# Adding expert results to their rows in DRAM by indirect accumulating transfers, in place of one-hot products

## The chip, the cores and the metric

The kernel runs on one core of a Trainium2 chip. Its time is the device time in microseconds. Three runs of the kernel before took 1575.61, 1576.45 and 1577.78, median 1576.45. Engines are named as in the profile: PE (TensorE, with PEld for its weight loads), DVE (VectorE), ACT (ScalarE), POOL (GpSimd), SP (SyncE). Transfers are issued from the queues of SP, ACT and POOL and carried out by 16 DMA engines.

## The reference

Two blocks run one after the other on a 512 x 1024 float32 activation. The first (mLSTM, convolution, feed-forward) and the attention parts of the second are not touched by the change. The last part of the second is a mixture of experts, and the change lies there:

```
def hierarchical_moe(h, w_group, b_group, w_expert, b_expert, w_gate, w_up, w_down):   # one row of 512 tokens
    g_sel = argmax(h @ w_group + b_group)                  # 1 of 4 groups per token
    e_logits = (h @ w_expert)[of the group]                # 8 experts in a group, 32 in all
    top_idx = top_k(e_logits + e_bias, 2)                  # 2 experts of that group per token
    gate = one_hot(g_sel) * normalised top-2 weights * g_w # 512 x 32
    a, u = h @ w_gate[e], h @ w_up[e]                      # 1024 -> 256 for each expert e
    return sum over e of (silu(a) * u * gate[:, e]) @ w_down[e]   # 256 -> 1024
```

Its result is added to the 512 x 1024 residual `x`. The two experts of a token always lie in the same group of eight.

## The kernel before, in words

`moe` (line 1557) holds the residual in four row tiles `xs[0..3]` of 128 tokens (each 128 x 1024, 512 KB; they lie in a buffer that the profile calls `crossq_U`). The output product `cross_w_o` of the cross attention ends with `fin0` and `fin1`, which add to `xs`, form the router's logits (line 1612), and store the normalised input of the experts, without its row scale, into the DRAM tensor `hd` (line 1618, from ACT's queue).

Then 16 expert pairs are worked through, pair p being experts 2p and 2p + 1. Each expert has 64 slots, so that a pair fills the 128 partitions. `pos` holds for each token and expert its slot, counted from 1, or 0. An expert with more than 64 tokens would be taken up again in `overflow`. For a pair, with the time at which it is called in iteration i of the loop (lines 1689 to 1703):

- `pair_take` (called for pair i + 3): `slots` compares `pos` with a ramp, which gives a one-hot matrix of tokens and slots; `look` multiplies it with `parts` (token number, gates and row scale, split into three bf16 parts), so each slot knows its token and gate. `fetch` gathers the 128 rows from `hd` by an indirect transfer of POOL's queue. An empty slot reads row 0. `pair_gates` sums the three parts.
- `pair_flip` (for pair i + 1): eight transposes on PE give `xT`.
- `pair_up` (pair i): 16 float32 matmuls of 512 columns, with gate and up weights side by side; then silu on ACT and a product on DVE. Inside, at k = 4 and 7, the results of the pair before are added to `xs[0]` and `xs[1]`.
- `pair_turn`: two transposes give `aT`. After it come the additions to `xs[2]` and `xs[3]`.
- `pair_down`: eight float32 matmuls give 128 x 1024; `split` writes the result as a rounded high part (ACT, line 188) and a low part (DVE, line 189) into `y`.
- `pair_add`: `pair_back` compares a ramp of token numbers with the token of each slot (line 1908); for each of the four row tiles and both halves two matmuls with this one-hot matrix (line 1901, high and low part) bring the slots back to their tokens, and DVE adds them to `xs` (line 1902). `pair_last` does it for the last pair by halves and stores the output (lines 1920 to 1922).

The weights of a pair are 12 pieces of 128 x 1024 float32 (512 KB): 8 of gate and up, 4 of down, in the order of their use (`ORDER`). `prefetch` issues them on SP's queue (line 1745) into a ring of places, piece n into place n modulo their number; a piece waits for the products that read the place before. Places become known step by step: 14 early, 11 in `hook`, 8 more before routing, 33 in all. The order on each engine is that in which the program calls these functions; nothing reorders it.

An accumulating transfer is also used in the first block: `weight` (line 138) writes a low part of a weight as copy of the negated high part (ACT) plus an accumulating transfer of the raw weight from SBUF to SBUF on POOL's queue, 512 KB each.

Of the kernel before, what the change touches and what calls it, by code (L numbers as in the profile page):

```python
# [11 lines left out]
F32 = mybir.dt.float32  # L12
F32R = mybir.dt.float32r
BF16 = mybir.dt.bfloat16
I32 = mybir.dt.int32
AF = mybir.ActivationFunctionType
ALU = mybir.AluOpType
PSUM = bass.MemoryType.PSUM

P = 128  # L20
S = 512
# [25 lines left out]
class Kern:  # L47
# [1509 lines left out]
    def moe(self, pm, o, X):  # L1557
# [24 lines left out]

        self.hd = self.dr.tile([S, D], F32, tag="hd", name="hd")

        info = self.info = pm.tile([P, 4, 34], F32, tag="info", name="info")
        self.parts = pm.tile([P, 4, 34, 3], BF16, tag="parts", name="parts")
        for tb in range(4):
            nc.gpsimd.iota(info[:, tb, 32:33], pattern=[[1, 1]], base=tb * P, channel_multiplier=1,
                           allow_small_or_imprecise_dtypes=True)
        self.split3(self.parts[:, :, 32:33], info[:, :, 32:33])  # L1590
        lg = pm.tile([P, 4, 36], F32, tag="lg", name="lg")

        half = {}

        def logits(tb, h):

            c = slice(h * 512, (h + 1) * 512)
            x = self.xs[tb][:, c]
            ss = self.small(1)
            self.sumsq(x, ss)  # L1600
            ps = self.psB()
            for k in range(4):
                nc.tensor.transpose(ps[:, k * P:(k + 1) * P], x[:, k * P:(k + 1) * P], self.ident)
            if tb == 3 and h == 1:
                dd = self.psB()
                for _ in range(1):
                    nc.tensor.matmul(dd[:, :256], self.ident, x[:, :256], start=True, stop=True)
            hT = pm.tile([P, 4, P], F32, tag="xg", bufs=2, name=self.nm("hT"))
            nc.scalar.copy(hT.rearrange("p k c -> p (k c)"), ps)
            pl = self.psB()  # L1610
            for k in range(4):
                nc.tensor.matmul(pl[:, :36], hT[:, k], wr[:, 4 * h + k], start=k == 0, stop=k == 3)
            if tb == 3 and h == 1:
                for _ in range(1):
                    nc.tensor.matmul(dd[:, :256], self.ident, x[:, :256], start=True, stop=True)
            t = self.tA()
            nc.vector.tensor_tensor(t, x, grow[:, c], op=ALU.mult)
            nc.scalar.dma_start(self.hd[tb * P:(tb + 1) * P, c], t)
            return ss, pl

        def fin0(tb, bank):
# [26 lines left out]
        def route(tbs):  # L1648
            self.places_of(tbs)
            t = slice(tbs[0], tbs[-1] + 1)  # L1650
            self.slots(oh[:, t], self.pos[:, t, 0:2])

        rest = Halves([])

# [22 lines left out]
        self.pair_collect(st[0], oh, (2, 3))  # L1677
        for p in range(3):
            st[p] = st.get(p, {})
            st[p]["oh"] = self.slots(self.slot_tile(), pos[:, :, 2 * p:2 * p + 2])  # L1680
            if p:
                self.fetch(st[p], self.look(st[p]["oh"], self.parts[:, :, 32:33]))
        self.gates_to(info[:, :, 0:32], pm, lg)
        self.split3(self.parts[:, :, 0:32], info[:, :, 0:32])
        self.split3(self.parts[:, :, 33:34], info[:, :, 33:34])
        for p in range(3):
            self.pair_gates(st[p], self.look(st[p]["oh"], self.parts), (2 * p, 2 * p + 1, 32))
        nwin = self.more_windows(pm, mb, onb)
        for i in range(16):
            prev = st.pop(i - 1) if i else None  # L1690
            self.pair_up(st[i], self.pair_weights(i), prev)
            self.prefetch(12 * i + 8)
            if i + 1 < 16:
                self.pair_flip(st[i + 1])
            self.pair_turn(st[i])
            if prev:
                self.pair_add(prev, (2, 3))
            if i + 3 < 16:
                p = i + 3
                st[p] = self.pair_take(pos[:, :, 2 * p:2 * p + 2], self.parts, (2 * p, 2 * p + 1, 32))  # L1700
            if i < 15:
                self.pair_down(st[i], self.pair_weights(i))
                self.prefetch(12 * (i + 1))
        for h in range(2):
            self.pair_down(st[15], self.pair_weights(15), (h,))
            self.pair_last(st[15], h)
# [18 lines left out]
    def prefetch(self, used):  # L1725

        a = self.a
        free = used + len(self.places)
        while len(self.pieces) < min(free, 192 if free >= 192 else 188):
            n = len(self.pieces)  # L1730
            if n == 188:

                for n in range(188, 192):
                    self.pieces.append(self.places[n % len(self.places)])
                for h in range(2):
                    for n in range(188, 192):
                        j, i = self.ORDER[n % 12]
                        c = slice(h * 512, (h + 1) * 512)
                        self.nc.sync.dma_start(self.pieces[n][:, c], a["w_dn"][30 + j, (i - 4) * P:(i - 3) * P, c])
                break  # L1740
            j, i = self.ORDER[n % 12]
            e = n // 12 * 2 + j
            src = a["w_gu"][e, i] if i < 4 else a["w_dn"][e, (i - 4) * P:(i - 3) * P, :]
            t = self.places[n % len(self.places)]
            self.nc.sync.dma_start(t, src)
            self.pieces.append(t)
# [17 lines left out]

    def slot_tile(self):
        return self.p0.tile([P, 4, 2, 64], BF16, tag="tB", bufs=4, name=self.nm("oh"))

    def slots(self, oh, pos):

# [26 lines left out]
    def fetch(self, s, tk):  # L1796

        nc = self.nc
        tf = self.small(1)
        nc.vector.tensor_reduce(tf, tk, axis=mybir.AxisListType.X, op=ALU.add)  # L1800
        ti = self.small(1, dt=I32)
        nc.vector.tensor_copy(ti, tf)
        xg = s["xg"] = self.pm.tile([P, 1024], F32, tag="xg", bufs=2, name=self.nm("xg"))
        nc.gpsimd.indirect_dma_start(out=xg, out_offset=None, in_=self.hd,
                                     in_offset=bass.IndirectOffsetOnAxis(ap=ti, axis=0))

    def pair_gates(self, s, ps, cols):

        nc = self.nc
        X = mybir.AxisListType.X  # L1810
        gt = s["gt"] = self.p0.tile([P, 3], F32, tag="gt", bufs=5, name=self.nm("gt"))
        nc.vector.tensor_reduce(gt[:, 1:3], ps[:, cols[2]:cols[2] + 2], axis=X, op=ALU.add)
        for j in range(2):
            r = slice(64 * j, 64 * j + 64)
            nc.vector.tensor_reduce(gt[r, 0:1], ps[r, cols[j]:cols[j] + 1], axis=X, op=ALU.add)
        nc.vector.tensor_tensor(gt[:, 0:1], gt[:, 0:1], gt[:, 2:3], op=ALU.mult)

    def pair_take(self, pos, parts, cols):

# [30 lines left out]
    def pair_flip(self, s):  # L1850
        s["xT"] = self.flip(s["xg"])

    def pair_up(self, s, w, prev=None):

        nc, pm = self.nc, self.pm
        ps = self.psA()
        for k in range(8):
            if prev and k in (4, 7):
                self.pair_add(prev, (0 if k == 4 else 1,))
            for j in range(2):  # L1860
                r = slice(64 * j, 64 * j + 64)
                nc.tensor.matmul(ps[r, :], s["xT"][:, k, r], w[j][k // 2][:, (k % 2) * 512:(k % 2 + 1) * 512], start=k == 0, stop=k == 7)  # L1862
        sl = pm.tile([P, 256], F32, tag="sl", bufs=2, name=self.nm("sl"))
        nc.scalar.activation(sl, ps[:, :256], AF.Silu, scale=s["gt"][:, 2:3])  # L1864
        nc.vector.scalar_tensor_tensor(sl, sl, s["gt"][:, 0:1], ps[:, 256:], op0=ALU.mult, op1=ALU.mult)
        s["sl"] = sl
# [7 lines left out]
        aT = s["aT"] = pm.tile([P, 2, P], F32, tag="aT", bufs=2, name=self.nm("aT"))  # L1874
        nc.vector.tensor_copy(aT.rearrange("p a b -> p (a b)"), pt[:, :256])

    def pair_down(self, s, w, hs=(0, 1)):
        nc, pm = self.nc, self.pm
        if hs[0] == 0:
            s["y"] = pm.tile([P, 2, 1024], F32R, tag="y", name=self.nm("y"))  # L1880
        y = s["y"]
        pd = {h: self.psA() for h in hs}
        for f in range(2):
            for h in hs:
# [2 lines left out]
                    nc.tensor.matmul(pd[h][r, :], s["aT"][:, f, r], w[j][4 + f][:, h * 512:(h + 1) * 512], start=f == 0, stop=f == 1)  # L1887
        for h in hs:
            c = slice(h * 512, (h + 1) * 512)
            self.split(y[:, 0, c], y[:, 1, c], pd[h])  # L1890

    def pair_add(self, s, tbs=range(4)):

# [50 lines left out]
    def overflow(self, pm, nwin):  # L1944
# [3 lines left out]
        with tc.If(n > 0):  # L1948
            pd = self.dr.tile([16, P, 4, 6], F32, tag="pd", name="pd")
            st = pm.tile([P, 4, 6], F32, tag="ofst", bufs=2, name="ofst")  # L1950
            for p in range(16):
                nc.vector.tensor_copy(st[:, :, 0:2], self.pos[:, :, 2 * p:2 * p + 2])
                nc.vector.tensor_copy(st[:, :, 2:4], self.info[:, :, 2 * p:2 * p + 2])
                nc.vector.tensor_copy(st[:, :, 4:6], self.info[:, :, 32:34])
                nc.sync.dma_start(pd[p], st)
            base = pm.tile([P, 1], F32, tag="base", name="base")
            nc.vector.memset(base, 0.0)
            with tc.For_i(0, n, 1):
                nc.vector.tensor_scalar(base, base, 64.0, None, op0=ALU.add)
                with tc.For_i(0, 16, 1) as p:  # L1960
# [3 lines left out]
                    for j in range(2):  # L1964
                        for i in range(6):
                            t = self.places[j * 6 + i]
                            if i < 4:
                                src = a["w_gu"][bass.ds(2 * p + j, 1), i]
                            else:
                                src = a["w_dn"][bass.ds(2 * p + j, 1), (i - 4) * P:(i - 3) * P]  # L1970
                            nc.sync.dma_start(t, src.rearrange("a p c -> (a p) c"))
                            ow[j][i] = t
                    nc.vector.tensor_scalar(st[:, :, 0:2], st[:, :, 0:2], base, None, op0=ALU.subtract)
# [144 lines left out]
```

## Time and profile before

| | us |
|---|---|
| median of three runs | 1576.45 (1575.61 to 1577.78) |
| the profiled execution | 1578.05 |
| its span in the profile | 1576.3 |
| PE busy | 1523.0 (97%) |
| DVE busy | 1030.9 (65%) |
| ACT busy | 681.4 (43%) |
| POOL busy | 107.2 (7%) |

The span runs from the first instruction to the last; start and end of the program around it make up the rest of the time. The pair loop lies between about 1282 and 1576 us of the span. PE's busy time counts pipelined matmuls, so a busy PE isn't PE at its peak. "PEclk" is the clock granted to PE as a share of 2.4 GHz. "DMA share" is the mean busy share of the 16 DMA engines by the durations of their packets, which can overlap, so it can lie a little above 1. In the span 313.39 MB were moved, 199 GB/s in the mean.

### The profile page before, as it was taken

The numbers are of one execution on the slowest core, as the hardware profiler recorded it, in microseconds if no ns is written. First come the engines' busy times: TensorE is split into PE (matmuls) and PEld (weight loads), VectorE is DVE, ScalarE is ACT, GpSimd is POOL, SyncE is SP. The second block draws the span as 40 slices with busy tenths as digits, with TensorE's granted clock in tenths as the row PEclk, the third lists the DMA queues.
The fourth block names the chain that finished last, engine by engine and source line by source line (L and its number), as shares of the span: only waits on it lengthen the run. The fifth ranks groups of instructions, "written<-read, shape, count | busy, mean of one in ns | idle before, by whom it ended". The sixth has DMA issues, their size and how long they took to land.

```text
span 1576.3 us, 20234 instructions
## 1 busy us (share of the span) xinstructions
PE 1523.0 (97%) x7272; PEld 1115.0 (71%) x7272; DVE 1030.9 (65%) x2192; ACT 681.4 (43%) x1227; POOL 107.2 (7%) x137
## 2 busy tenths in 40 slices
PE   7999999999999999999999999999999989999997
PEld 4667777778888888888888877788777854444432
DVE  4578999976857855555336687847667385565543
ACT  5544576567847644444325463444355221111110
POOL 1111111111000000000000010101011010000000
PEclk9999999999999999999999999999999999999999
DMA  9899977866275433223446532532334789999931
GB/s 326 297 273 262 268 177 192 254 155 154 101 270 190 142 94 95 93 95 96 142 134 200 163 106 84 184 101 80 132 109 167 280 297 387 413 417 414 417 132 55
DMA packets 90585, 313.39 MB, mean 199 GB/s; under 512 B 10608, under 2 KB 11120, under 8 KB 90480
## 3 DMA queue, kind: packets, MB, share of 16 engines
q1 hardware_dynamic: 77808, 268.00, 48.4%
q0 software_dynamic: 9792, 35.66, 10.2%
q10 hardware_dynamic: 2880, 8.39, 1.4%
q8 instruction: 58, 0.95, 0.3%
q14 instruction: 47, 0.39, 0.1%
HBM read 271.64 MB, written 14.68 MB: 182 GB/s over the span
## 4 chain that ended last, share of the span: by engine, by line
PE 77%; DMA 8%; DVE 8%; ACT 3%; issue 2%; POOL 2%; SPq 0%; ACTq 0%; DVEq 0%; POOLq 0%
PE moe_pa L1862 7%; PE up_pa L148 5%; PE up_pa L147 5%; PE up_pa L146 5%; PE moe_pb L1901 4%; PE moe_pa L1887 4%; DMA glu_raw<-in_w_in_dram 2%; DMA glu_w<-glu_raw 2%; PE vo_pa L146 2%; PE vo_pa L148 2%; PE vo_pa L147 2%; PE wout_pa L148 2%; PE wout_pa L146 2%; PE wout_pa L147 2%; PE qk_pa L146 1%
## 5 line engine op out<-in xcount | busy, mean ns | idle before, releaser
L632 DVE SCALAR_TENSOR_TENSOR y<-g,cols,y 128x493 f32<-128x493 f32 (+26 forms) x240 | 165.7, 728 | 9.8 <-ACT y L629 8.1
L148 PE MATMUL up_pa<-u,up_w 128*128 128x512 f32 (+1 forms) x384 | 145.6, 380 | 0.0
L147 PE MATMUL up_pa<-u,up_w 128*128 128x512 f32 (+1 forms) x384 | 144.1, 376 | 0.4 <-DVE u L189 0.4
L146 PE MATMUL up_pa<-u,up_w 128*128 128x512 f32 (+1 forms) x384 | 143.2, 374 | 0.3 <-ACT u L188 0.3
L1902 DVE TENSOR_TENSOR crossq_U<-crossq_U,moe_pb 128x512 f32<-128x512 f32 x120 | 75.9, 681 | 84.4 <-PE moe_pb L1901 84.4
L919 DVE SCALAR_TENSOR_TENSOR up_tA<-up_pa,cols,up_tA 128x511 f32<-128x511 f32 x88 | 65.7, 748 | 78.7 <-ACT up_tA L917 77.3
L147 PEld LDWEIGHTS up_pa<-u,up_w 128*128 128x128 f32 x384 | 72.1, 188 | 16.3 <-DVE u L189 0.6
L146 PEld LDWEIGHTS up_pa<-u,up_w 128*128 128x128 f32 x384 | 71.9, 188 | 15.5 <-ACT u L188 1.1
L148 PEld LDWEIGHTS up_pa<-u,up_w 128*128 128x128 f32 x384 | 72.2, 188 | 13.7
L141 DVE TENSOR_TENSOR down_w<-down_raw,down_w 128x1024 fp32r<-128x1024 f32 x36 | 42.8, 1221 | 56.0 <-ACT down_w L135 56.0
L141 DVE TENSOR_TENSOR wout_w<-wout_raw,wout_w 128x512 fp32r<-128x512 f32 (+1 forms) x72 | 51.3, 745 | 35.1 <-ACT wout_w L135 35.0
L1901 PE MATMUL moe_pb<-moe_y,moe_back 128*128 128x512 f32 x240 | 72.8, 421 | 0.7 <-ACT moe_y L188 0.7
L1864 ACT ACTIVATE moe_sl<-moe_pa,moe_gt 128x256 f32<-128x256 f32 x16 | 7.6, 473 | 147.0 <-PE moe_pa L1862 147.0
L1901 PEld LDWEIGHTS moe_pb<-moe_y,moe_back 128*128 128x128 f32 x240 | 41.4, 188 | 37.5 <-issue 25.1
L917 ACT ACTIVATE up_tA<-up_pa,cols 128x512 f32<-128x512 f32 x44 | 34.2, 778 | 72.7 <-PE up_pa L148 72.7
L135 ACT CAST down_w<-down_raw 128x1024 fp32r<-128x1024 f32 x36 | 36.4, 1049 | 65.0 <-PE down_pb L148 33.7
L135 ACT CAST wout_w<-wout_raw 128x512 fp32r<-128x512 f32 (+1 forms) x72 | 44.9, 670 | 44.6 <-PE wout_pa L148 21.5
L141 DVE TENSOR_TENSOR up_w<-up_raw,up_w 128x1024 fp32r<-128x1024 f32 (+1 forms) x48 | 54.0, 1127 | 0.2 <-ACT up_w L135 0.2
L188 ACT CAST moe_y<-moe_pa 128x512 fp32r<-128x512 f32 x32 | 18.6, 586 | 82.3 <-PE moe_pa L1887 82.3
L146 PE MATMUL glu_pa<-mem_U,glu_w 128*128 128x512 f32 x128 | 50.9, 401 | 2.8 <-ACT mem_U L188 2.8
L147 PE MATMUL g_pa<-g_w,down_U 128*128 128x512 f32 x128 | 51.0, 399 | 0.5 <-DVE g_w L141 0.5
L146 PE MATMUL g_pa<-g_w,down_U 128*128 128x512 f32 x128 | 51.4, 403 | 0.0
(747 smaller groups left out, 4066.4 us busy)
## 6 DMA issues: line engine op xcount, KB each, us to landing
up_raw<-in_ffn_up_dram SPq DMA_DIRECT2D x44, 512.0 KB
wout_raw<-in_w_out_dram SPq DMA_DIRECT2D x40, 512.0 KB
down_raw<-in_ffn_down_dram SPq DMA_DIRECT2D x36, 512.0 KB
ew<-in_w_gu_dram SPq DMA_DIRECT2D x35, 512.0 KB
glu_U<-in_ada_w_dram SPq DMA_DIRECT2D x32, 512.0 KB
wo_ew<-in_w_gu_dram SPq DMA_DIRECT2D x17, 512.0 KB
mem_raw<-in_w_kv_dram SPq DMA_DIRECT2D x16, 512.0 KB
mem_aw<-in_ada_w_dram SPq DMA_DIRECT2D x16, 512.0 KB
```

Of the source, the lines that this page charges most:

```text
L135: nc.scalar.copy(w[:, 0, c], raw[:, c])
L141: nc.vector.tensor_tensor(w[:, 1, c], raw[:, c], w[:, 0, c].bitcast(F32), op=ALU.subtract)
L146: mm(out, lh, rh, start=start, stop=False)
L147: mm(out, lh, rl, start=False, stop=False)
L148: mm(out, ll, rh, start=False, stop=stop)
L632: nc.vector.scalar_tensor_tensor(acc[:, s:], g[:, :512 - s], cw[:, j:j + 1], acc[:, s:], op0=ALU.mult, op1=ALU.add)
L917: nc.scalar.activation(acc, pq, AF.Identity, scale=cwv(2), bias=self.col("ffn_conv_b", cc))
L919: nc.vector.scalar_tensor_tensor(acc[:, s:], pq[:, :512 - s], cwv(2 - s), acc[:, s:], op0=ALU.mult, op1=ALU.add)
L1862: nc.tensor.matmul(ps[r, :], s["xT"][:, k, r], w[j][k // 2][:, (k % 2) * 512:(k % 2 + 1) * 512], start=k == 0, stop=k == 7)
L1887: nc.tensor.matmul(pd[h][r, :], s["aT"][:, f, r], w[j][4 + f][:, h * 512:(h + 1) * 512], start=f == 0, stop=f == 1)
L1901: nc.tensor.matmul(pc, back[:, tb * P:(tb + 1) * P], y[:, i, c], start=i == 0, stop=i == 1)
L1902: nc.vector.tensor_tensor(self.xs[tb][:, c], self.xs[tb][:, c], pc, op=ALU.add)
```

## The change

15 of the 16 pairs no longer add their results to `xs` on PE and DVE. A second DRAM tensor `sums` (512 rows and 128 spare ones) gets a copy of `x` while the router's logits are formed. Each pair's result is copied to one of two tiles `yt` and added to its tokens' rows of `sums` by an indirect accumulating transfer of POOL's queue; an empty slot adds to the spare row of its partition. After the loop the 512 rows are read back into `xs`, and the last pair is added to them as before. So that a row occurs once in a transfer, pair p is now experts p and p + 16, which belong to different groups. Token numbers are carried 1024 lower and raised again, so an empty slot (sum 0) points to row 1024 and the gather leaves it out (bounds check). `xs` is free during the loop, and its four tiles are added to the places.

```
+        self.sums = self.dr.tile([S + P, D], F32, tag="sums", name="sums")
...
-            nc.gpsimd.iota(info[:, tb, 32:33], pattern=[[1, 1]], base=tb * P, channel_multiplier=1,
+            nc.gpsimd.iota(info[:, tb, 32:33], pattern=[[1, 1]], base=tb * P - 1024, channel_multiplier=1,
...
+        nc.gpsimd.iota(self.spare, pattern=[[1, 1]], base=S - 1024, channel_multiplier=1, allow_small_or_imprecise_dtypes=True)
...
             nc.scalar.dma_start(self.hd[tb * P:(tb + 1) * P, c], t)
+            nc.scalar.dma_start(self.sums[tb * P:(tb + 1) * P, c], x)
...
         nwin = self.more_windows(pm, mb, onb)
+
+        xs = self.xs
+        self.places += xs
+        self.prefetch(0)
+        yt = pm.tile([P, 2, 1024], F32, tag="y", name="yt")
         for i in range(16):
-            prev = st.pop(i - 1) if i else None
-            self.pair_up(st[i], self.pair_weights(i), prev)
+            self.pair_up(st[i], self.pair_weights(i))
             self.prefetch(12 * i + 8)
             if i + 1 < 16:
                 self.pair_flip(st[i + 1])
             self.pair_turn(st[i])
-            if prev:
-                self.pair_add(prev, (2, 3))
             if i + 3 < 16:
                 p = i + 3
-                st[p] = self.pair_take(pos[:, :, 2 * p:2 * p + 2], self.parts, (2 * p, 2 * p + 1, 32))
+                st[p] = self.pair_take(self.pair_pos(p), self.parts, (p, p + 16, 32))
             if i < 15:
-                self.pair_down(st[i], self.pair_weights(i))
+                self.pair_down(st[i], self.pair_weights(i), out=yt[:, i % 2])
                 self.prefetch(12 * (i + 1))
+                self.pair_scatter(st[i], yt[:, i % 2])
+        for tb in range(4):
+            nc.sync.dma_start(xs[tb], self.sums[tb * P:(tb + 1) * P, :])
...
-        nc.vector.tensor_copy(ti, tf)
+        nc.vector.tensor_scalar(ti, tf, 1024.0, None, op0=ALU.add)
...
-                                     in_offset=bass.IndirectOffsetOnAxis(ap=ti, axis=0))
+                                     in_offset=bass.IndirectOffsetOnAxis(ap=ti, axis=0), bounds_check=S - 1, oob_is_err=False)
...
+        e = self.small(1)
+        nc.vector.tensor_scalar(e, gt[:, 1:2], 0.0, self.spare, op0=ALU.is_equal, op1=ALU.mult)
+        nc.vector.tensor_scalar(gt[:, 1:2], gt[:, 1:2], 1024.0, None, op0=ALU.add)
+        to = s["to"] = self.small(1, dt=I32)
+        nc.vector.tensor_tensor(to, gt[:, 1:2], e, op=ALU.add)
...
-            self.split(y[:, 0, c], y[:, 1, c], pd[h])
+            if out is None:
+                self.split(y[:, 0, c], y[:, 1, c], pd[h])
+            else:
+                (nc.vector.tensor_copy if h else nc.scalar.copy)(out[:, c], pd[h])
+
+    def pair_scatter(self, s, y):
+
+        self.nc.gpsimd.indirect_dma_start(out=self.sums, out_offset=bass.IndirectOffsetOnAxis(ap=s["to"], axis=0), in_=y,
+                                          in_offset=None, bounds_check=S + P - 1, compute_op=ALU.add)
```

`pair_pos(p)` gives the two columns p and p + 16 of `pos`; the sources of the weights are numbered likewise. `overflow` follows the new numbering.

## Rows read from the trace of the kernel before

**Rows 1.** The chain of waits in the pair loop: start us, us, what.
```profile
1301.83 3.43 PE moe_pa L1862 x16
...
1400.19 3.43 PE moe_pa L1862 x16
1403.62 1.14 PE moe_pb L1901 x4
1404.75 2.73 PE moe_pa L1862 x12
1407.48 1.13 PE moe_pb L1901 x4
1408.61 1.01 PE moe_pa L1862 x4
1409.62 1.02 PE moe_pb L1761 x8
1411.17 1.63 PE moe_pb L1901 x7
1413.00 3.58 PE moe_pa L1887 x16
1416.58 3.43 PE moe_pa L1862 x16
```

**Rows 2.** Busy time by stretch: length, engines' us, PEclk, DMA share, GB/s.
```profile
1240.00:1250.00 10.00, 10.00 (x64) 8.87 (x63) 3.23 (x9) 3.43 (x6) 0.00 (x0) 1.00 0.37 115
...
1280.00:1285.00 5.00, 5.00 (x42) 3.40 (x42) 3.89 (x18) 0.06 (x1) 0.00 (x0) 1.00 0.13 50
...
1295.00:1300.00 5.00, 3.71 (x12) 1.26 (x14) 4.79 (x18) 0.06 (x1) 0.94 (x1) 0.66 1.03 410
1300.00:1305.00 5.00, 5.00 (x26) 1.50 (x22) 2.03 (x4) 1.17 (x2) 0.00 (x0) 1.00 0.91 302
...
1350.00:1360.00 10.00, 10.00 (x46) 3.59 (x42) 3.83 (x7) 1.17 (x2) 0.38 (x1) 1.00 1.03 419
...
1480.00:1490.00 10.00, 10.00 (x46) 3.56 (x42) 3.31 (x7) 1.17 (x2) 0.94 (x1) 1.00 1.02 415
...
1508.00:1512.00 4.00, 4.00 (x22) 2.56 (x19) 2.45 (x6) 1.06 (x2) 0.00 (x0) 1.00 0.57 217
1512.00:1516.00 4.00, 4.00 (x19) 1.24 (x17) 1.80 (x4) 0.62 (x2) 0.00 (x0) 1.00 0.00 0
```

**Rows 3.** Waits of SP's queue after 1200: total us, times, longest.
```profile
SPq L1745 <- PE moe_pa L1887: 64.4, 29, 8.4
...
SPq L1745 <- PE moe_pa L1862: 51.2, 48, 10.8
```

**Rows 4.** Groups of instructions in 1318 to 1514: busy us, mean ns, idle before.
```profile
L1902 DVE TENSOR_TENSOR crossq_U<-crossq_U,moe_pb 128x512 f32<-128x512 f32 x96 | 60.4, 681 | 64.2 <-PE moe_pb L1901 64.2
...
L1908 DVE TENSOR_SCALAR moe_back<-iotat,moe_gt 128x512 fp32r<-128x512 f32 x11 | 5.3, 486 | 0.4
```

**Rows 5.** Timeline of SP's queue: the first issue into a freed place.
```profile
1284.48 2.04 SPq L1745 DMA_DIRECT2D ew<-in_w_dn_dram  x3
```

**Rows 6.** Transfers in 1300 to 1500 (packets, MB, share); gathers' landing.
```profile
q0 software_dynamic: 1707, 6.21, 7.9%
...
DMA to landing us min/median/max: 5.5/7.6/9.1
```

**Rows 7.** Transfers in 120 to 160; landing of the accumulating ones.
```profile
q1 hardware_dynamic: 1920, 6.99, 51.2%
q0 software_dynamic: 932, 3.42, 45.3%
...
DMA to landing us min/median/max: 4.4/7.9/11.4
```

**Rows 8.** Timeline of the last subtraction and the last additions.
```profile
1565.42 0.69 DVE L189 TENSOR_TENSOR moe_y<-moe_pa,moe_y 128x512 fp32r<-128x512 f32 x1 [0.93 <-ACT moe_y L188]
...
1566.90 2.48 DVE L1921 TENSOR_TENSOR crossq_U<-crossq_U,moe_pb 128x512 f32<-128x512 f32 x4 [0.79 <-PE moe_pb L1920]
```

**Rows 9.** Timeline of PE: the transposes of pair 1.
```profile
1293.38 1.06 PE L1761 MATMUL moe_pb<-ident,moe_xg 128*128 128x128 f32 x8 [2.02 <-DMA moe_xg<-hd,moe_sm]
```

More of the change, by code (lines that the diff above doesn't have):

```diff
@@ L1587, in moe @@
         for tb in range(4):
-            nc.gpsimd.iota(info[:, tb, 32:33], pattern=[[1, 1]], base=tb * P, channel_multiplier=1,
+            nc.gpsimd.iota(info[:, tb, 32:33], pattern=[[1, 1]], base=tb * P - 1024, channel_multiplier=1,
                            allow_small_or_imprecise_dtypes=True)
         self.split3(self.parts[:, :, 32:33], info[:, :, 32:33])
+        self.spare = pm.tile([P, 1], F32, tag="spare", name="spare")
+        nc.gpsimd.iota(self.spare, pattern=[[1, 1]], base=S - 1024, channel_multiplier=1, allow_small_or_imprecise_dtypes=True)
         lg = pm.tile([P, 4, 36], F32, tag="lg", name="lg")
@@ L1650, in route @@
             t = slice(tbs[0], tbs[-1] + 1)
-            self.slots(oh[:, t], self.pos[:, t, 0:2])
+            self.slots(oh[:, t], self.pair_pos(0)[:, t])
         rest = Halves([])
@@ L1679, in moe @@
             st[p] = st.get(p, {})
-            st[p]["oh"] = self.slots(self.slot_tile(), pos[:, :, 2 * p:2 * p + 2])
+            st[p]["oh"] = self.slots(self.slot_tile(), self.pair_pos(p))
             if p:
@@ L1686, in moe @@
         for p in range(3):
-            self.pair_gates(st[p], self.look(st[p]["oh"], self.parts), (2 * p, 2 * p + 1, 32))
+            self.pair_gates(st[p], self.look(st[p]["oh"], self.parts), (p, p + 16, 32))
         nwin = self.more_windows(pm, mb, onb)
+        xs = self.xs
+        self.places += xs
+        self.prefetch(0)
+        yt = pm.tile([P, 2, 1024], F32, tag="y", name="yt")
         for i in range(16):
-            prev = st.pop(i - 1) if i else None
-            self.pair_up(st[i], self.pair_weights(i), prev)
+            self.pair_up(st[i], self.pair_weights(i))
             self.prefetch(12 * i + 8)
@@ L1738, in prefetch @@
                         c = slice(h * 512, (h + 1) * 512)
-                        self.nc.sync.dma_start(self.pieces[n][:, c], a["w_dn"][30 + j, (i - 4) * P:(i - 3) * P, c])
+                        self.nc.sync.dma_start(self.pieces[n][:, c], a["w_dn"][15 + 16 * j, (i - 4) * P:(i - 3) * P, c])
                 break
             j, i = self.ORDER[n % 12]
-            e = n // 12 * 2 + j
+            e = n // 12 + 16 * j
             src = a["w_gu"][e, i] if i < 4 else a["w_dn"][e, (i - 4) * P:(i - 3) * P, :]
@@ L1766, in slot_tile, with pair_pos @@
         return self.p0.tile([P, 4, 2, 64], BF16, tag="tB", bufs=4, name=self.nm("oh"))
+    def pair_pos(self, p):
+        return self.pos.rearrange("p t (j e) -> p t e j", j=2)[:, :, p]
     def slots(self, oh, pos):
@@ L1851, in pair_flip, with pair_up @@
         s["xT"] = self.flip(s["xg"])
-    def pair_up(self, s, w, prev=None):
+    def pair_up(self, s, w):
         nc, pm = self.nc, self.pm
@@ L1857, in pair_up @@
         for k in range(8):
-            if prev and k in (4, 7):
-                self.pair_add(prev, (0 if k == 4 else 1,))
             for j in range(2):
@@ L1875, in pair_turn, with pair_down @@
         nc.vector.tensor_copy(aT.rearrange("p a b -> p (a b)"), pt[:, :256])
-    def pair_down(self, s, w, hs=(0, 1)):
+    def pair_down(self, s, w, hs=(0, 1), out=None):
         nc, pm = self.nc, self.pm
-        if hs[0] == 0:
+        if hs[0] == 0 and out is None:
             s["y"] = pm.tile([P, 2, 1024], F32R, tag="y", name=self.nm("y"))
-        y = s["y"]
+        y = s.get("y")
         pd = {h: self.psA() for h in hs}
@@ L1951, in overflow @@
             for p in range(16):
-                nc.vector.tensor_copy(st[:, :, 0:2], self.pos[:, :, 2 * p:2 * p + 2])
-                nc.vector.tensor_copy(st[:, :, 2:4], self.info[:, :, 2 * p:2 * p + 2])
+                nc.vector.tensor_copy(st[:, :, 0:2], self.pair_pos(p))
+                nc.vector.tensor_copy(st[:, :, 2:4], self.info[:, :, 0:32].rearrange("p t (j e) -> p t e j", j=2)[:, :, p])
                 nc.vector.tensor_copy(st[:, :, 4:6], self.info[:, :, 32:34])
@@ L1967, in overflow @@
                             if i < 4:
-                                src = a["w_gu"][bass.ds(2 * p + j, 1), i]
+                                src = a["w_gu"][bass.ds(p + 16 * j, 1), i]
                             else:
-                                src = a["w_dn"][bass.ds(2 * p + j, 1), (i - 4) * P:(i - 3) * P]
+                                src = a["w_dn"][bass.ds(p + 16 * j, 1), (i - 4) * P:(i - 3) * P]
                             nc.sync.dma_start(t, src.rearrange("a p c -> (a p) c"))
```

## The prediction

> **What bounds the kernel now.** The chain of waits comes first: in the pair loop it stays on PE, and a pair repeats every 16.39 us, 1400.19 to 1416.58 [rows 1]. In one period the up products take 3.43 + 2.73 + 1.01 = 7.17 us, the down products 3.58, the transposes of the next pair 1.02, and the one-hot products of line 1901 1.14 + 1.13 + 1.63 plus one more ahead of the transposes of line 1873, about 4.05. The rest is those transposes, the slot look-up and hand-overs.
>
> The second view is the busy time by stretch. In the same loop the 16 DMA engines show a share of 1.03 at 419 GB/s [rows 2]: 12 weight pieces of 524,288 bytes and a gather of as many are 6.82 MB in 16.39 us, 416 GB/s. PE and the transfers are thus both full. Which leads is told by SyncE's waits: its issues of weights stood 64.4 and 51.2 us for down and up products to give places free [rows 3]. So PE sets the pace; the loads run ahead by the 33 places. They end near 1510 (217 GB/s in 1508 to 1512, then nothing), and the last 66 us of the span need no weights at all [rows 2]. That is the room that a faster PE can use, and no more: it can't finish before its weights.
>
> **The change part by part.** Differences are taken on the profiled span, 1576.3; that execution took 1578.05, so 1.75 lie outside it, and it is 1.6 above the median of 1576.45. I carry the difference to the median.
>
> *Removed.* 15 pairs lose 16 one-hot products each, about 4.05 us of PE, with the eight DVE additions of 0.681 us and one comparison of 0.486 [rows 4], and one cast and one subtraction become two copies. What is late next on PE: the products of line 1901 covered the silu, its product and the transposes; I add 0.7 us of wait, so a pair needs 16.39 - 4.05 + 0.7 = 13.0 us of PE. Alone that would take 15 x 3.4 = 50 us off, an end near 1526.
>
> *Transfers, which are now late.* After 1280 the DMA engines stand almost idle (50 GB/s): all 33 places are full and the next 159 pieces wait for the first up products at 1284.48 [rows 2, 5]. The four row tiles, now further places, let loads start about 2 us sooner; I take 1282.5. From there:
> - Weights: 159 x 524,288 / 417 GB/s (between the 415 and 419 of two stretches [rows 2]) = 159 x 1.257 = 199.9 us.
> - Gathers: a gather of 128 rows took 7.9% of 200 us for 6.21 MB, 1.33 us per 0.524 MB [rows 6]. 512 tokens with two experts fill 1024 of 2048 slots, so with empty slots left out half the rows go: 15 x 0.67 = 10.0.
> - Scatters: 15 of 128 rows each, full or not, since empty slots go to spare rows. No row shows an accumulating transfer into DRAM. The nearest is the accumulating one from SBUF into SBUF of the first stage, same queue, same 512 KB. In 120 to 160 that queue used 45.3% of 40 us for 3.42 MB, 2.78 us per 512 KB, over twice a load. Charged with everything that plain loads lost beside it, it is (0.965 x 40 - 6.99 MB / 417 GB/s) / 6.52 = 3.35 us [rows 7]. I take 3.1, between the two, since the loop has twelve loads to one accumulation and that stretch only two: 46.5 us. Ends: as cheap as a plain transfer, 1.257 (it can't be less, its bytes still move), and with a separate read and write of DRAM on top, 3.1 + 2 x 1.257 = 5.6.
> - A gap near 1300, as now (302 GB/s for 5 us is 1.4 us lost) [rows 2]: 1.4.
>
> Sum 257.8: the last weights land at 1282.5 + 257.8 = 1540.3, 30 us later than before. Per pair the transfers need 15.1 + 0.7 + 3.1 = 18.9 us, more than the old period and far more than PE's 13.0. Pair 1 starts at 1301.8 as now [rows 1], with some 32 pieces in hand (33 and what has landed since 1282.5, less pair 0's 12); PE uses 12 / 13.0 = 0.92 per us and gets 12 / 18.9 = 0.64, so it has caught up 32 / 0.28 = 113 us later, near 1410, and waits for weights in every pair from there.
>
> The Trainium skill ("Collectives: The Full Stack", The bandwidth ceiling) says that an add in the transfer engine costs two source reads on one ring, so twice a copy, and there the operands lie in DRAM; by that estimate a scatter is 2.5 us and the time 1549. The trace's SBUF rows are a little dearer than that, and no run here shows the DRAM case.
>
> *The tail.* After the last weights come the four row tiles from the sums, 4 x 1.257 = 5.0 us behind them in the same queue, and 1.5 us for issue and landing. Scatter 14 ends earlier: its rows leave about when pair 14's last weights have landed, 12 pieces ahead (18 us), plus some 4 us of products and copies and 7.9 us to landing [rows 7]. Then one addition (0.62), the subtraction (0.69), a product (0.5), four additions (2.48), and 6.9 from the last addition to the end of the span [rows 8]: 17.7 in all. End 1558.0, 18.3 below 1576.3. In runs: 1576.45 - 18.3 = **1558**.
>
> *Costed at nothing.* The eight stores of the row tiles into the sums (2.1 MB, 5 us of transfers, eight more issues on ACT's queue beside those of line 1618): the engines were 0.37 used in 1240 to 1250 and stood idle after 1280 [rows 2]; without that cover up to 5 us. Three DVE instructions of one column more per pair: DVE loses 8 x 0.681 + 0.486 = 5.9 us there [rows 4]. On POOL a scatter waits for the copies and for the scatter before, and the next pair's gather stands behind it; that gather is needed two iterations later, and landings of 5.5 to 9.1 us (gather) and 4.4 to 11.4 (accumulation) [rows 6, 7] lie inside a period of 18.9. The two copy tiles come back after two pairs.
>
> **Rivals.**
> 1. *The scatter is dearer in DRAM (slower side).* Place: the transfer engines, in every pair. For it: transfers are already at a share of 1.03, so each microsecond per scatter is 15 on the end. Against: weights from DRAM move at 419 GB/s, so DRAM as such isn't slow. It decides from 3.1 + 18.3 / 15 = 4.3 us per scatter; at 5.6 the time is 1558 + 38 = 1596.
> 2. *The scatter costs no more than a plain transfer, or its second read hides.* 15 x 1.84 less: 1530. Against: the accumulating queue's share [rows 7].
> 3. *PE's clock falls while it waits.* From 1410 on PE waits about 6 us per pair. Where PE stood 2.02 us for a gather and then for short steps, the granted clock was 0.66 in 1295 to 1300 [rows 2, 9], so part of that was spent at 1.2 GHz. At that level throughout, a pair's 12.4 us of matmuls become 24.8, 25.4 with the hand-overs, and the 6.7 pairs left at 1410 end at 1580, the span at 1598. Against: a slow PE waits less, and full work went on at 1.00 [rows 2]. It costs nothing as long as those pairs average (1540.3 - 1410) / 6.7 = 19.4 us, a mean clock of 0.66, and turns the change slower from 22.2 us, below 0.57. The Trainium skill ("TensorE: Matmul & The Clock Gate", HAM oscillation) states this rule: tiles whose compute is shorter than the wait for their data start at the low clock each time; by it the loop would run as in this rival, and the trace agrees only for a single stall.
> 4. *The gather saves nothing* (left-out rows still cost a descriptor's time): 10 us more, 1568.
>
> **How the numbers follow.** Forecast (scatter between 2.5 and 3.7 us: 1549 to 1567) 0.46; rival 1 0.21; rival 2 and what lies between it and the forecast 0.17; rival 3 0.08; rival 4 0.08. About 0.2% (3 us) can't be told from no change. All of the forecast, rival 2 and rival 4 are faster, 0.71; a scatter between 4.1 and 4.5 us or a clock near 0.57 lands within 0.2%, 0.06; the rest, 0.23, is slower. The range takes in most of rival 2 (1532) and rivals 1 and 3 up to 5.0 us per scatter (1586).
>
> **What would show it.** Right: the transfer share stays at 1.0 until about 1540 with fewer GB/s than 417; PE waits for weights from near 1410, and SyncE's waits for PE shrink; the software queue takes some 55 us of the engines for its 15 scatters and gathers; the end lies 15 to 20 us behind the last weight. Wrong: PE full up to the end (transfers not the bound), engines idle in the loop (a wait of POOL or of a place instead), a software queue above 75 us, or a granted clock under 0.66 after 1410.

## The result and the profile after

The changed kernel takes 1558.74 us (median of 4 runs, 1556.00 to 1561.53) against 1576.03 of the kernel before on the same chip (4 runs, 1575.21 to 1577.78): 0.9888 of it (0.987 to 0.9906). Measured once more on another chip, in five rounds, it was 1555.93 against 1576.24, 0.9865 (0.9839 to 0.9892). The forecast was 1558, range 1532 to 1586. The execution whose trace follows spans 1554.3 us and took 1556.00, the quickest of the four.

The chain of waits of the kernel after (start us, us, what), to be held against [rows 1]:

```profile
1310.64 3.65 PE moe_pa L1906 x16
1314.30 6.92 PE moe_pa L1880 x32
1321.31 0.70 DVE moe_xT L1772
1323.46 3.65 PE moe_pa L1906 x16
...
1339.93 3.47 PE moe_pa L1880 x16
1343.40 13.36 DMA ew<-in_w_gu_dram
1356.82 13.33 DMA crossq_U<-in_w_dn_dram
...
1410.33 13.76 DMA ew<-in_w_gu_dram
```

The one-hot products are gone from PE, and while PE still leads, a pair repeats every 1323.46 - 1310.64 = 12.82 us, where it was 16.39. From 1343.40 on the chain runs mostly through weight loads. The bound has changed hands, as forecast.

Busy time by stretch of the kernel after, with the columns of [rows 2]:

```profile
1280.00:1285.00 5.00, 5.00 (x40) 2.97 (x40) 3.98 (x22) 0.34 (x2) 0.25 (x1) 1.00 0.97 343
1295.00:1300.00 5.00, 5.00 (x26) 2.86 (x26) 4.17 (x24) 0.00 (x0) 1.27 (x1) 0.66 0.73 274
1300.00:1305.00 5.00, 5.00 (x26) 1.64 (x24) 1.84 (x5) 0.58 (x1) 2.90 (x2) 1.00 0.91 289
1320.00:1350.00 30.00, 28.09 (x147) 10.96 (x145) 10.56 (x39) 4.02 (x8) 6.07 (x5) 1.00 1.04 364
1400.00:1420.00 20.00, 16.81 (x71) 5.99 (x71) 3.33 (x13) 1.53 (x3) 2.63 (x2) 1.00 1.03 391
1420.00:1440.00 20.00, 16.65 (x66) 5.98 (x65) 3.33 (x13) 1.53 (x3) 2.62 (x2) 0.83 1.03 391
1480.00:1500.00 20.00, 17.18 (x70) 6.48 (x68) 3.70 (x7) 2.48 (x5) 1.57 (x1) 0.93 1.03 391
1540.00:1545.00 5.00, 3.92 (x12) 1.39 (x9) 3.20 (x6) 0.58 (x1) 0.00 (x0) 1.00 0.35 134
```

Three things are to be seen. The transfers stay at a share of 1.03 to 1.04 but move 364 to 391 GB/s in the stretches from 1320 to 1500 shown, instead of 415 to 419: the engines are as full as before, on bytes that take longer. PE, which filled every stretch of [rows 2] from 1300 on, is busy 16.7 to 17.2 of 20 us in 1400 to 1440 and in 1480 to 1500. And the work in 1280 to 1285, a share of 0.13 before, is 0.97 now; the stretch without transfers at the end is gone, since they now run to about 1541.

SyncE's waits after 1200 in the kernel after (us in total, times, longest), beside [rows 3]:

```profile
SPq L1755 <- DMA ew<-in_w_gu_dram: 24.8, 17, 3.1
SPq L1755 <- DMA moe_ew<-in_w_gu_dram: 23.9, 17, 3.5
...
SPq L1755 <- PE moe_pa L1906: 13.0, 14, 8.5
```

Its wait for the down products (L1887 before, L1906 now), 64.4 us before, is 13.0. The largest are now waits for earlier loads, by which the issues follow the transfers.

Transfers of the kernel after in 1340 to 1500 (packets, MB, share of the 16 engines):

```profile
DMA packets 17480, 61.39 MB, mean 384 GB/s; under 512 B 2514, under 2 KB 2514, under 8 KB 17471
...
q1 hardware_dynamic: 14735, 53.66, 82.8%
q0 software_dynamic: 2736, 7.62, 20.3%
```

The software queue, 7.4% of this stretch before with gathers of whole tiles alone, has a fifth of the engines.

### The profile page after: what moved, and what is told of

It is laid out like the page before. It is cut to its first block, busy times and chain, and to the rows that moved or that the text cites. A ratio compares the mean times of both kernels' runs of the same rounds, so it can differ in the third digit from the quotient of the medians.

```text
span 1554.3 us, 19779 instructions
## 1 busy us (share of the span) xinstructions
PE 1475.9 (95%) x7032; PEld 1084.6 (70%) x7032; DVE 947.2 (61%) x2090; ACT 671.3 (43%) x1212; POOL 132.4 (9%) x153
## 4 chain that ended last, share of the span: by engine, by line
PE 67%; DMA 16%; DVE 10%; ACT 2%; issue 2%; POOL 2%; SPq 0%; DVEq 0%; ACTq 0%; POOLq 0%
PE up_pa L148 5%; PE up_pa L147 5%; PE up_pa L146 5%; DMA ew<-in_w_gu_dram 3%; PE moe_pa L1880 2%; DVE y L632 2%; PE vo_pa L146 2%; PE vo_pa L148 2%; PE vo_pa L147 2%; PE wout_pa L148 2%; DMA moe_ew<-in_w_gu_dram 2%; PE wout_pa L146 2%; PE wout_pa L147 2%; DMA glu_raw<-in_w_in_dram 2%; DMA crossq_U<-in_w_dn_dram 2%
## 5 line engine op out<-in xcount | busy, mean ns | idle before, releaser
L1772 DVE COPY moe_xT<-moe_pb 128x512 f32<-128x512 f32 x15 | 10.4, 692 | 124.3 <-PE moe_pa L1880 122.8
L146 PE MATMUL glu_pa<-mem_U,glu_w 128*128 128x512 f32 x128 | 51.1, 402 | 4.4 <-ACT mem_U L188 4.4
L147 PE MATMUL g_pa<-g_w,down_U 128*128 128x512 f32 x128 | 51.0, 398 | 0.5 <-DVE g_w L141 0.5
L146 PE MATMUL g_pa<-g_w,down_U 128*128 128x512 f32 x128 | 51.4, 402 | 0.0
L147 PE MATMUL glu_pa<-mem_U,glu_w 128*128 128x512 f32 x128 | 50.5, 396 | 0.4 <-DVE mem_U L189 0.4
L148 PE MATMUL g_pa<-g_w,down_U 128*128 128x512 f32 x128 | 50.7, 396 | 0.0
L148 PE MATMUL glu_pa<-mem_U,glu_w 128*128 128x512 f32 x128 | 50.4, 395 | 0.0
```

The lines of the kernel that those rows point to most:

```text
L146: mm(out, lh, rh, start=start, stop=False)
L147: mm(out, lh, rl, start=False, stop=False)
L148: mm(out, ll, rh, start=False, stop=stop)
L1772: (nc.scalar.copy if i else nc.vector.tensor_copy)(t[:, i * 4:i * 4 + 4].rearrange("p k c -> p (k c)"), ps)
```

## The experiments

Theory A is the prediction's: PE set the pace before, the transfers do after, and a scatter costs them some 3 us. A ratio is to the kernel before, run on the same chip. The changed kernel's own two ratios, 0.9888 and 0.9865, are both used below, so differences have two values; 0.001 is 1.58 us, or 0.105 us for each of 15 scatters.

**No scatter.**

```
-                self.pair_scatter(st[i], yt[:, i % 2])
```

> The changed kernel with its 15 accumulating transfers left out (the results of 15 pairs are then missing from the output). Theory A (the 16 DMA engines set the pace from the point where PE has used up its lead, and a scatter takes about 2.7 us of them): 15 x 2.7 = 40 us less, but PE's own need of 12.8 us per pair sets a floor near 1512, so 1515 to 1522. Rival B (the scatter's time hides, the loads or PE's hand-overs set the pace): no change, 1556 to 1561. Rival C (the clock falls while PE waits and that is what costs): PE would wait less here, so the time falls too, but only by what the slower stretches cost, some 5 us.

1518.09 us, 0.9623 (0.9603 to 0.9643), as theory A said. So 15 scatters cost the kernel 38 to 42 us, 2.5 to 2.8 each. Its transfers in 1340 to 1500:

```profile
DMA packets 19313, 65.98 MB, mean 412 GB/s; under 512 B 2718, under 2 KB 2718, under 8 KB 19302
...
q1 hardware_dynamic: 18050, 63.62, 98.2%
q0 software_dynamic: 1252, 2.22, 3.6%
```

Even without scatters the transfers remain full, at 412 GB/s. But they no longer lead. The chain of waits of this kernel runs on PE and its hand-overs from 1300 to the end, no load is in it, and in 1300 to 1500 PE has no wait for a weight:

```profile
1459.05 6.88 PE moe_pa L1879 x32
...
1471.88 6.88 PE moe_pa L1879 x32
```

A pair repeats here after 12.83 us, as while PE led in the changed kernel. The time is thus PE's own need, the floor that the expectation names, and 2.5 to 2.8 us is the least that a scatter took of the transfers. The gathers have 3.6% of 160 us for 2.22 MB, which is 8.5 of 0.262 MB: 0.68 us each, the 0.67 of the prediction.

**A scatter that writes and does not add.** The edit drops the addition from the same transfer:

```
-  in_offset=None, bounds_check=S + P - 1, compute_op=ALU.add)
+  in_offset=None, bounds_check=S + P - 1)
```

> The 15 scatters write their rows plainly instead of adding to them (the output then keeps only the last writer of a row). Theory A with an accumulation priced as two reads and a write: a plain one takes 1.3 us of the engines, so 15 x 1.4 = 21 us less, about 1538. Rival D (what costs is that rows are scattered into DRAM one by one, the addition is free): no change, 1556 to 1561. Rival B: no change either.

1535.42 us, 0.9728 (0.9708 to 0.9747). Against no scatter that is 1.1 us for a plain one (again the least, since PE sets the end without scatters), against the changed kernel 1.4 to 1.7 us for the addition. The same view of this kernel:

```profile
DMA packets 18957, 66.80 MB, mean 418 GB/s; under 512 B 2670, under 2 KB 2670, under 8 KB 18947
...
q1 hardware_dynamic: 16133, 58.75, 90.1%
q0 software_dynamic: 2814, 7.93, 12.4%
```

The plain scatter runs at the full 418 GB/s. By the software queue's share, 19.8 us for eleven scatters and eight gathers by their bytes, a plain one takes (19.8 - 8 x 0.68) / 11 = 1.3 us, no more than a load of as many bytes (1.257). It is the addition that makes the same bytes take some two times as long, and not the indirect addressing. Rival 2 (as cheap as a plain transfer) falls here, and so does rival 1 (5.6).

**Empty slots left out of the scatter too.**

```
-        nc.vector.tensor_scalar(e, gt[:, 1:2], 0.0, self.spare, op0=ALU.is_equal, op1=ALU.mult)
...
-        nc.vector.tensor_tensor(to, gt[:, 1:2], e, op=ALU.add)
+        nc.vector.tensor_copy(to, gt[:, 1:2])
-  in_offset=None, bounds_check=S + P - 1, compute_op=ALU.add)
+  in_offset=None, bounds_check=S - 1, oob_is_err=False, compute_op=ALU.add)
```

> Empty slots are left out of the scatter by its bounds check, as they are left out of the gather, instead of being added to spare rows; the output stays complete. Theory A: half the rows (64 of 128 on average) leave, 15 x 1.35 = 20 us less, 1536 to 1541, faster than both kernels. Rival E (a left-out row still takes its share of the engines): no change, 1556 to 1561. Rival B: no change.

1545.12 us, 0.9787 (0.9759 to 0.9816): faster, but by less than half the price of a scatter, and not the 1536 to 1541 expected. Its transfers in 1340 to 1500 show a part of the reason:

```profile
DMA packets 18273, 61.50 MB, mean 384 GB/s; under 512 B 3279, under 2 KB 3279, under 8 KB 18265
...
q1 hardware_dynamic: 15551, 56.62, 89.0%
q0 software_dynamic: 2714, 4.78, 12.2%
```

The software queue has about as many packets as in the changed kernel (2714 and 2736) with 2.84 MB less in them, and in all there are 3279 under 512 B where there were 2514: a row left out still goes through the queue as a small packet.

**All rows gathered again.**

```
-        nc.vector.tensor_scalar(ti, tf, 1024.0, None, op0=ALU.add)
+        nc.vector.tensor_scalar(ti, tf, 1024.0, 511.0, op0=ALU.add, op1=ALU.min)
```

> The gather fetches all 128 rows again; an empty slot reads row 511 and its result goes to a spare row as before. Theory A with a gather of 64 rows at 0.67 us and of 128 at 1.33: 15 x 0.67 = 10 us more, 1567 to 1571. Rival E (left-out rows cost as much as gathered ones) or B: no change, 1556 to 1561.

1564.90 us, 0.9918 (0.9901 to 0.9934): 5 to 8 us slower than the changed kernel, where 10 were expected. Leaving rows out of the gather does pay, so rival 4 falls, and a whole gather seems cheaper than [rows 6] made it: 0.68 + 5 / 15 to 0.68 + 8 / 15 = 1.0 to 1.2 us, not 1.33. This is likely and not settled: the interval touches that of the first measurement of the changed kernel (0.9901 and 0.9906).

**More work for PE.** Four products of 512 columns added to each pair, their result unused:

```
+            if k in (4, 7):
+                dd = self.psB()
+                for _ in range(2):
+                    nc.tensor.matmul(dd, self.ident, self.iotat, start=True, stop=True)
```

> The changed kernel with four more 512-column float32 matmuls per pair inside the up products, whose result nobody reads: some 3.6 us of PE per pair, about what the change took away. Theory A: PE's need rises from 12.8 to about 16.4 us per pair and stays below the 18 us of the transfers, so at most the last pair's share is seen, 1558 to 1564. Rival F (PE and its hand-overs still set the pace after the change): 16 x 3.6 = 58 us more, near 1616.

1563.88 us, 0.9909 (0.9889 to 0.993). The rival of a PE that still leads would have added the whole 16 x 3.6 = 58 us; 3 to 7 were added. In this kernel PE is full again and the transfers stay full beside it:

```profile
1320.00:1340.00 20.00, 20.00 (x86) 6.87 (x84) 3.71 (x14) 1.65 (x3) 4.49 (x3) 1.00 1.03 390
1400.00:1420.00 20.00, 20.00 (x87) 6.96 (x84) 4.35 (x15) 1.65 (x3) 4.50 (x3) 1.00 1.03 388
```

Its chain of waits is on PE again, and from 1302 to the end no load is in it:

```profile
1302.38 3.43 PE moe_pa L1884 x16
...
1497.36 3.43 PE moe_pa L1884 x16
```

Twelve pairs lie between these two, 16.25 us each, where a pair of the changed kernel took 12.82 while PE led: 3.4 us more per pair, 55 over 16 pairs. So in the changed kernel some 3 us of PE per pair are free, and hardly more: with 3.4 added PE leads again. The expectation had the time right and this not: it held PE's 16.4 us per pair against the transfers' 18 and left out the pieces that are loaded ahead, for which PE need not wait.

**The halved gather alone, in the kernel before.** The index and bound of the changed gather, with the one-hot products kept:

```
-                                     in_offset=bass.IndirectOffsetOnAxis(ap=ti, axis=0))
+                                     in_offset=bass.IndirectOffsetOnAxis(ap=ti, axis=0), bounds_check=S - 1, oob_is_err=False)
```

> The kernel before with only the gather's part of the change: empty slots aren't gathered, results are still added by one-hot products on PE. Theory A: before the change PE sets the pace and the transfers run ahead of it, so no change, 1574 to 1579. Rival G (the kernel before was already bound by its transfers): 5 to 10 us less.

1577.93 us, 1.000 (0.999 to 1.001). The transfers were as full as PE before, yet relieving them gives nothing: PE led, as its being waited for had said [rows 3].

**Filled slots spread over the tile.** Like the third, and the slots of an expert are numbered so that the filled ones lie apart (a table of 8 is kept in the old order for its other use):

```
-  nc.gpsimd.iota(self.iota1, pattern=[[1, 64]], base=1, ...
+  nc.gpsimd.iota(self.iota1, pattern=[[1, 8], [8, 2], [16, 2], [32, 2]], base=1, ...
```

> As the run that leaves empty slots out of the scatter, and in addition the filled slots of an expert are spread over its 64 partitions (slot numbers dealt out in an interleaved order) instead of lying in the first ones; the same rows and bytes move. Theory H (a transfer with half its rows left out loads few of the 16 engines, and the weights wait for the fullest engine; so left-out rows gave back only 1.06 us per scatter and 0.3 per gather where halves would be 1.35 and 0.67): 15 x 0.65 = 10 us less than that run, about 1535. Rival E (a left-out row still costs its engines some time): no change from that run, about 1545.

1542.01 us, 0.9775 (0.9751 to 0.9799), between the two expectations; by itself it doesn't tell them apart.

**The four row tiles not used as places.**

```
-        self.places += xs
```

> The changed kernel without the four row tiles as further places for weights (33 places as before). Theory A: the transfer engines stand idle from about 1280 to 1284 as before the change, and four pieces less are in flight, so 2 to 5 us more, 1560 to 1564. Rival (the places matter throughout because PE frees them late): more than 10 us.

1566.71 us, 0.9933 (0.9916 to 0.9949), 7 to 11 us slower than the changed kernel, where the prediction had counted 2 and the expectation 2 to 5. Three stretches of this kernel show where:

```profile
1280.00:1290.00 10.00, 10.00 (x69) 5.96 (x70) 8.42 (x42) 0.34 (x2) 2.18 (x2) 1.00 0.52 181
1290.00:1300.00 10.00, 6.84 (x52) 3.91 (x51) 7.06 (x45) 2.34 (x3) 0.39 (x1) 0.92 0.96 363
1300.00:1310.00 10.00, 10.00 (x44) 3.14 (x42) 3.63 (x16) 0.59 (x1) 3.78 (x3) 0.91 0.76 244
```

and the same three of the changed kernel:

```profile
1280.00:1290.00 10.00, 10.00 (x72) 5.04 (x71) 8.18 (x48) 0.73 (x3) 2.18 (x2) 1.00 0.99 347
1290.00:1300.00 10.00, 7.31 (x40) 4.26 (x40) 7.53 (x45) 1.95 (x3) 1.27 (x1) 0.83 0.88 343
1300.00:1310.00 10.00, 10.00 (x58) 4.23 (x54) 3.35 (x12) 1.53 (x3) 2.90 (x2) 1.00 0.94 299
```

Without the places the engines lose 4.7 us (0.99 - 0.52) in the first stretch and 1.8 in the third, and win 0.8 in the second: 5.7 in all, and 2.0 MB less are moved, about four pieces. The first issue into a place that PE frees is late as well:

```profile
1285.78 2.04 SPq L1754 DMA_DIRECT2D ew<-in_w_dn_dram  x3
```

It comes 1.3 us after that of the kernel before [rows 5] and 1.9 after the changed kernel's (1283.90, shown below); why is not shown. So not all of the 7 to 11 us need be the places'.

**The three best on one chip.** The changed kernel, the one without empty slots and the one with spread slots, five rounds each:

> The changed kernel itself once more, so that the two after it can be set against it on one chip. All theories: 0.987 to 0.991 of the kernel before.

> The kernel that leaves empty slots out of the scatter, once more, with more rounds. Theory A with the cost of a half scatter as read from its first trace (1.9 us against 2.5 to 2.8): 0.6 to 0.9 us less per scatter, 9 to 14 us less than the changed kernel, 0.980 of the kernel before. Rival E in full (left-out rows cost as much as others): the same as the changed kernel.

> The kernel with empty slots left out of the scatter and the filled ones spread over the partitions, once more, with more rounds. Theory H, sized by the rates of the two first traces (394 against 384 GB/s with the engines' share at 1.03 against 1.01): 3 to 6 us less than the run without the spreading, 0.976 to 0.978 of the kernel before. Rival E: the same as without it, 0.980.

1555.93, 1547.16 and 1540.86 us: 0.9865 (0.9839 to 0.9892), 0.981 (0.9785 to 0.9834), 0.9775 (0.9752 to 0.9797). What tells the last two apart are the queues' lines of 1340 to 1500, for the one without empty slots,

```profile
q1 hardware_dynamic: 15574, 56.71, 89.3%
q0 software_dynamic: 2758, 4.90, 12.3%
```

and with spread slots:

```profile
q1 hardware_dynamic: 15777, 57.45, 89.4%
q0 software_dynamic: 2880, 5.19, 13.2%
```

With spread slots more weights pass in the same time, 57.45 against 56.71 MB, and in the earlier two runs 58.01 against 56.62. The two executions traced here took 1549.41 and 1550.14 us, each the longest of its kernel, so these lines stand for less than the medians' difference. What is left of the 160 us after weights at 1.257 us per piece and gathers at 0.68 is 1.7 to 1.8 us per scatter with packed slots and 1.4 to 1.5 with spread ones (eleven scatters by their bytes, perhaps twelve in the last); the same working gives 2.5 in the changed kernel, with ten. Half of 2.5 to 2.8 is 1.25 to 1.4. So spreading seems to give back most of what leaving out fell short by. The order of the medians was the same both times, 3 and 6 us, but the intervals of both pairs overlap: likely, not settled. That a share of the engines stood idle while others held the filled rows is the argument for it; no row here shows single engines.

The kernel with spread slots is the fastest of those that add every result, 0.9775 of before in both measurements.

## Why the prediction was right

**What bounds.** Right on both sides of the change: the halved gather alone gave nothing before, and added PE work cost little after. The margin is small, though: PE leads again without the scatters, and with 3.4 us more of PE per pair.

**PE's pair.** Forecast 13.0 us, measured 12.82. The step "has caught up near 1410" was late. PE's waits for weights, first within 1380 to 1420 of the kernel after,

```profile
PE moe_pa L1880 <- DMA moe_ew<-in_w_gu_dram: 1.8, 2, 1.3
```

and then within 1420 to 1535,

```profile
PE moe_pa L1880 <- DMA ew<-in_w_gu_dram: 6.1, 4, 2.4
...
PE moe_pa L1880 <- DMA moe_ew<-in_w_gu_dram: 4.2, 3, 2.1
```

begin some 10 to 30 us before 1410 (1300 to 1380 has none of PE's own). It costs nothing: the loads set the end.

**The scatter.** Taken at 3.1 us, it is at least 2.5 to 2.8 by the times. By the queue's share in 1300 to 1500 of the kernel after,

```profile
q0 software_dynamic: 3711, 10.04, 21.4%
```

42.8 us are 13 scatters and 12 gathers by their bytes, and less 12 x 0.68 a scatter is 2.7. The accumulating row from SBUF [rows 7] was thus the right one to go by, and its lower reading (2.78, the share) the nearer. The term of 46.5 us was 5 to 8 us too large. The estimate of 2.5 from the Trainium skill ("Collectives: The Full Stack", The bandwidth ceiling: an add reads two sources, so twice the traffic) lies at the lower end of what was measured, and the two-fold price agrees with 1.1 to 1.3 plain and 2.5 to 2.8 adding. The forecast by it, 1549, was still the worse one, for the other terms did not hold exactly.

**The start of the loads.** This step failed in size: "let loads start about 2 us sooner". SyncE's queue in the kernel after:

```profile
1276.57 5.43 SPq L1755 DMA_DIRECT2D crossq_U<-in_w_dn_dram  x3
1282.16 0.33 SPq L1755 DMA_DIRECT2D crossq_U<-in_w_gu_dram  x1
1283.90 5.48 SPq L1755 DMA_DIRECT2D ew<-in_w_gu_dram  x7
```

The four places were issued from 1276.57, eight microseconds before [rows 5], and their four transfers of 1.26 us bridge to the first place that PE frees. What I missed is that four more places are four more pieces in front of a standstill, 5 us of transfers, whatever the instant at which they begin. Against the forecast's own start the gain was smaller: 343 GB/s in 1280 to 1285 are 3.3 pieces, a start at 1282.5 allows 2.0, so the loads were some 1.3 pieces, 1.6 us, ahead of it. The eight stores into the sums, costed at nothing, did not hold them up.

**The gap near 1300.** Taken as before at 1.4 us lost; 274 and 289 GB/s in 1295 to 1305 are 5 x (1 - 274 / 417) + 5 x (1 - 289 / 417) = 3.2. By the shares of 0.73 and 0.91 against a full 1.03 it is 2.0; the rest may be the first scatter, counted above.

**The tail.** The chain of waits of the kernel after has its last load here,

```profile
1519.38 10.90 DMA ew<-in_w_gu_dram
...
1530.33 1.95 PE moe_pa L1880 x6
```

and in its timeline DVE waits once for a row tile:

```profile
1538.39 0.69 DVE L1948 TENSOR_TENSOR crossq_U<-crossq_U,moe_pb 128x512 f32<-128x512 f32 x1 [0.72 <-DMA crossq_U<-sums]
```

The last weights, eight half pieces of which the last is issued at 1530.3 and takes 6.7 us to arrive, landed near 1537, 3 us before the forecast's 1540.3. From there the span has 17.3 us, forecast 17.7. But the path was another one. The last load in the chain ends at 1530.3, with the last piece of the gate and up weights, and from there the chain runs through the last pair's own products, copies and additions, 24 us to the end; the only wait for a row tile is 0.72 us, and it isn't in the chain. The forecast had the end wait for the four row tiles. Both paths come out nearly equal here, so that 17.7 fits is in part luck.

**The sum.** The span came out 3.7 us below the 1558.0 worked out for it. Scatters took 5 to 8 off and the places 1.6 more; the gap gave 0.6 to 1.8 back. That would put the last weights 5 to 9 below, where they were 3 early, so 2 to 6 us of transfers are not accounted for; the last loads at 314 GB/s in 1530 to 1535 may hold 1.2 of them. That the median of the runs agrees with the forecast within 1 us is partly errors that cancel and a spread of 5 us between runs.

**The clock.** Rival 3 did not decide. The granted clock was 0.83 in 1420 to 1440 and 0.93 in 1480 to 1500, and 1.00 in 1400 to 1420, though PE stood idle some 3 us in each 20 (rival 3 counted 6 in each pair; why PE shows busier than its own 12.82 us per pair is not settled here); all are above the 0.66 at which it would have begun to cost. The rule that rival 3 takes from the Trainium skill speaks of work shorter than the wait; the 12.4 us of matmuls of a pair are longer than the 6 us of wait that rival 3 itself counts, so the loop was not such a case to begin with.

## What to carry to other kernels

When two engines are both full, the waits say which one leads: here only relief of that one paid, and only up to the next one's own time. Work moved from TensorE into accumulating transfers should be priced, by these runs, at two times its bytes or a little more, and tiles that come free with the change are worth their bytes wherever loads stand still for want of a place.

## What the runs showed of the hardware

An accumulating scatter of 128 rows, 512 KB, into DRAM took the transfer engines at least 2.5 to 2.8 us (2.7 by the queue's share) where a plain one took 1.1 to 1.3, and held GpSimd longer as well. The groups of GpSimd after 1300, of the changed kernel,

```profile
L1916 POOL DMA_INDIRECT sums<-yt,moe_sm x15 | 23.8, 1589 | 100.2 <-DVE yt L1912 68.4 <-DMA ew<-in_w_gu_dram 17.0 <-ACT yt L1912 8.3
```

and with the plain scatter:

```profile
L1916 POOL DMA_INDIRECT sums<-yt,moe_sm x15 | 15.3, 1018 | 92.0 <-DVE yt L1912 69.5 <-DMA ew<-in_w_gu_dram 12.9 <-ACT yt L1912 8.3
```

1.59 us of GpSimd against 1.02, both well inside a pair. And rows left out of an indirect transfer don't give back their whole price: half of the rows gave back 9 to 16 us over 15 scatters, where half of the price would be 19 to 21, and 14 to 18 with the filled slots spread. How much of the rest is the small packets and how much the packing of the slots is not settled.
